# A new instruction order for four engines of a cosine-similarity attention kernel

## The chip, the cores and the metric

The kernel runs on one core of a Trainium2 chip. The metric is the device time of one execution in microseconds (us), as a median over repeated runs. The kernel before takes 190.19 us (median of 3 runs, 190.16 to 190.32).

## What is computed

Q, K and V have 8 batches of 12 heads, each 512 x 64 in float32.

```python
Q_norm = Q / (np.linalg.norm(Q, axis=-1, keepdims=True) + 1e-10)
K_norm = K / (np.linalg.norm(K, axis=-1, keepdims=True) + 1e-10)
scores = np.einsum('bhqd,bhkd->bhqk', Q_norm, K_norm) / tau        # tau = 0.1
weights = np.exp(scores - np.max(scores, axis=-1, keepdims=True))
weights = weights / (np.sum(weights, axis=-1, keepdims=True) + 1e-10)
return np.einsum('bhqk,bhkd->bhqd', weights, V)
```

Scores of normalised rows lie between -10 and 10, so the kernel leaves out the maximum.

## The kernel before

The 96 heads are worked off as 48 pairs of heads, numbered 0 to 47. Each pair goes through the same chain of small operations, and each operation has a key, which this document writes as a name with numbers: `EXP 5.2` is the exponential of pair 5, key block 2.

| name | engine | what it does | line |
|---|---|---|---|
| LD s.0, LD s.1, LV s | SP queue | loads Q, K (256 KB each) and V of pair s | L315, L318 |
| SQ s.0 | POOL (GpSimd) | squares of Q and K | L341 |
| SSQ s.1 | PE (TensorE) | eight matmuls that add up the squares of K, in part | L358 |
| RED s.0, RED s.1 | DVE (VectorE) | row sums of the squares: of Q over the whole (L369), of K over what SSQ left (L365) | L369, L365 |
| NEW g.0 to g.8 | DVE | inverse square root for a group g of 1, 2 or 4 pairs, in small steps, nearly each of which reads what the one before it wrote | L394 to L403 |
| SCL s.0, SCL s.1 | DVE, POOL | Q and K of pair s times their inverse norms; Q on DVE, K on POOL (in nine pairs on DVE) | L427 |
| TR s.0, TR s.1 | PE | four transposes each | L433 |
| EVA s | DVE | copies the transposed pair from PSUM to SBUF | L441 |
| SCO s.c | PE | two matmuls: scores of key block c, for both heads | L532 |
| EXP s.c | ACT (ScalarE) | exponential of that block, 128x1024 | L548 |
| VC s | POOL | V to bf16 | L553 |
| PV s.h.i | PE | four matmuls: weights times V for head h, query block i | L565 |
| RCP s.h, NRM s.h | DVE | one over the sum of the weights; the output times it | L576, L578 |
| ST s | SP queue | stores the pair (256 KB) | L582 |

Some dependences matter below. SCO needs a free one of two double banks of scores, so `SCO n` waits until the exponential two places before it has ended. `SCO s.0` needs EVA s, which needs TR s.0 and TR s.1, which need SCL s.0 and SCL s.1, and these need NEW, RED and SQ. A PV chain has one bank for each head: `PV s.h.0` needs NRM s-1.h. `NRM s` writes into one of eight output buffers and needs the store ST s-8 to have landed. An SQ writes into one of six buffers, and a load LD s into one of 17, so LD s waits for SCL s-17.

Each engine works through a list of operations in a fixed order, and an operation that waits holds up all that stand behind it on that engine or queue. The lists stand in the program as numbers, in the constant `ORDER`, one text for each of sp, pool, dve, pe and act. `schedule` turns the numbers into operations, and `run` works out the semaphores from the operations' needs. Costs and due times that the operations carry are no longer used for the order. Before the first pair stands a head (pair 0 and the first operations of pairs 1 to 3), with warm-up matmuls and fillers on PE.

Of the kernel before, what the change touches and what calls it, by code (L numbers as in the profile page):

```python
# [669 lines left out]
def slack(s, most):  # L670
# [13 lines left out]
    ),  # L684
    "pool": (
# [7 lines left out]
    ),  # L693
    "dve": (
# [23 lines left out]
    ),  # L718
# [78 lines left out]
```

## Time and profile before

| | |
|---|---|
| median of 3 runs | 190.19 us |
| span of the profiled execution | 189.9 us |
| first and last start of EXP on 128x1024 (186 of them) | 12.9 and 184.5 us |
| loads and stores | 50.76 MB, 267 GB/s over the span |

A page of the profile gives the busy time of each engine, the span cut in 40 slices with the busy tenths of each and the granted clock of PE ("PEclk"), the chain of work that ended last, and groups of instructions. A row of a group reads: line, engine, operation, output <- inputs, shapes, xcount | busy us, mean ns of one | idle time of the engine just before them and what ended it. A row of a timeline reads: start in us, duration in us, engine, line, operation, tiles, shapes, xcount, and in brackets an idle time of the engine before it with what ended it. Neighbours of one kind are merged into one row. A row of the windows gives a stretch, its length, and then the busy us and number of instructions of PE, PEld (weight loads), DVE, ACT and POOL, and last the granted clock, the share of the DMA engines and GB/s. A row of a line's own view gives the number of its instructions, their shortest, median and longest duration in ns, and the first and last start.

### The profile page before, as it was taken

To read this page: it belongs to the slowest core of one execution; us is meant where nothing else is said; L and a number is where in the kernel's file an instruction comes from. 1 tells how busy PE (TensorE), PEld (TensorE's weight loads), DVE (VectorE), ACT (ScalarE), POOL (GpSimd) and SP (SyncE) were. 2 spreads that over 40 slices of the span, in tenths; PEclk is the share of its full clock that TensorE was granted. 3 is DMA by queue.
4 is the path that set the end of the run, shared out by engine and by line. 5 is a ranking of instruction groups with operands and counts; after the bars stand their busy time and mean duration, and the time that the engine had idled before them with its cause. 6 is when DMAs were issued, how large, how long until landed. Compare 5 with 4: busy or idle time off the path is not lost.

```text
span 189.9 us, 6666 instructions
## 1 busy us (share of the span) xinstructions
PE 175.6 (92%) x2714; PEld 109.3 (58%) x2714; DVE 170.1 (90%) x552; ACT 183.0 (96%) x215; POOL 161.7 (85%) x150
## 2 busy tenths in 40 slices
PE   7989699999999999999899999899999899897973
PEld 2555356656655666666566566566656565464642
DVE  2699979999999999999997998999999999988642
ACT  5799989999999999999999999999999999999994
POOL 5599987999999999999999999999999994893000
PEclk9999879999999999999999999999999999999999
DMA  5999999999994789999979999999950414000555
GB/s 157 340 358 348 347 349 373 364 369 293 324 384 166 209 270 344 358 369 374 370 238 284 325 383 368 358 366 364 383 200 5 166 59 166 3 0 3 198 194 166
DMA packets 52446, 50.76 MB, mean 267 GB/s; under 512 B 3136, under 2 KB 52416, under 8 KB 52416
## 3 DMA queue, kind: packets, MB, share of 16 engines
q1 hardware_dynamic: 51984, 50.02, 79.7%
q8 instruction: 21, 0.34, 0.7%
q10 hardware_dynamic: 432, 0.33, 0.5%
q14 instruction: 9, 0.07, 0.1%
HBM read 37.75 MB, written 12.58 MB: 265 GB/s over the span
## 4 chain that ended last, share of the span: by engine, by line
ACT 34%; POOL 28%; DVE 20%; PE 8%; DMA 3%; issue 3%; SPq 3%; POOLq 0%
ACT et L548 31%; POOL sq L341 16%; POOL qn L427 6%; POOL vb L553 5%; DVE qn L427 4%; DVE ob L578 3%; DMA out_dram<-ob 3%; DVE qt L441 3%; DVE nps L369 3%; PE scps L532 2%; PE ops L191 2%; ACT et L524 2%; PE ops L565 2%; SPq L315 1%; DVE rd L576 1%
## 5 line engine op out<-in xcount | busy, mean ns | idle before, releaser
L548 ACT ACTIVATE et<-scps 128x1024 bf16<-128x1024 f32 x186 | 171.8, 1104 | 0.8 <-PE scps L532 0.7
L341 POOL TENSOR_TENSOR sq<-qk 128x1024 bf16<-128x1024 f32 x44 | 83.2, 1900 | 0.1
L532 PE MATMUL scps<-qt 64*128 64x512 bf16 x374 | 73.6, 389 | 6.1 <-ACT et L548 3.4
L565 PE MATMUL ops<-vb,et 128*128 128x65 bf16 x1504 | 73.2, 195 | 1.8 <-DVE ob L578 1.2
L565 PEld LDWEIGHTS ops<-vb,et 128*128 128x128 bf16 x1504 | 55.7, 98 | 31.2 <-issue 18.1
L427 POOL TENSOR_TENSOR qn<-qk,rk 128x512 bf16<-128x512 f32 x38 | 39.5, 1048 | 5.8 <-PE scps L532 3.7
L578 DVE TENSOR_TENSOR ob<-ops,rd 128x256 f32<-128x256 f32 x94 | 38.6, 416 | 0.8
L427 DVE TENSOR_TENSOR qn<-qk,nps 128x512 bf16<-128x512 f32 x56 | 37.1, 675 | 0.7 <-ACT nps L386 0.6
L433 PE MATMUL tps<-ident,qn 128*128 128x128 bf16 x376 | 33.9, 221 | 1.1 <-POOL qn L427 0.5
L441 DVE COPY qt<-tps 128x1024 bf16<-128x1024 bf16 x47 | 32.0, 680 | 0.4 <-PE tps L433 0.4
L369 DVE TENSOR_REDUCE nps<-sq 128x8 f32<-128x512 bf16 x46 | 30.8, 681 | 1.0 <-POOL sq L341 0.8
L532 PEld LDWEIGHTS scps<-qt 64*128 64x128 bf16 x374 | 18.2, 93 | 23.4 <-ACT et L548 9.0
L553 POOL TENSOR_SCALAR vb<-vf 128x512 bf16<-128x512 f32 x48 | 29.8, 633 | 0.2 <-PE scps L532 0.2
L433 PEld LDWEIGHTS tps<-ident,qn 128*128 128x128 bf16 x376 | 21.7, 98 | 12.6 <-issue 6.0
L576 DVE RECIPROCAL rd<-ops 128x4 f32<-128x4 f32 x94 | 15.9, 173 | 6.9 <-PE ops L565 5.9
L358 PE MATMUL ops<-sq,ident 128*128 128x64 bf16 x384 | 19.0, 194 | 0.1
L358 PEld LDWEIGHTS ops<-sq,ident 128*128 128x128 bf16 x384 | 14.5, 98 | 2.7 <-issue 1.8
L365 DVE TENSOR_REDUCE nps<-ops 128x8 f32<-128x64 f32 x46 | 10.0, 217 | 0.6 <-PE ops L358 0.5
L394 DVE TENSOR_TENSOR nps<-nps,ys 128x32 f32<-128x32 f32 (+2 forms) x34 | 7.0, 207 | 0.4
L395 DVE SCALAR_TENSOR_TENSOR nps<-nps,ys 128x32 f32<-128x32 f32 (+2 forms) x34 | 7.0, 206 | 0.4
L335 POOL TENSOR_TENSOR sq<-qk 128x512 bf16<-128x512 f32 (+1 forms) x5 | 4.7, 955 | 2.2 <-DMA qk<-in_K_dram 1.9
L191 PE MATMUL ops<-warm_in,ident 128*128 128x512 bf16 x8 | 3.6, 631 | 1.4 <-POOL eps L184 1.4
(66 smaller groups left out, 61.2 us busy)
## 6 DMA issues: line engine op xcount, KB each, us to landing
vf<-in_V_dram SPq DMA_DIRECT2D x48, 256.0 KB, 6.5
qk<-in_Q_dram SPq DMA_DIRECT2D x47, 256.0 KB, 5.5
qk<-in_K_dram SPq DMA_DIRECT2D x47, 256.0 KB, 6.5
out_dram<-ob SPq DMA_DIRECT2D x47, 256.0 KB, 5.8
qk<-in_Q_dram SPq DMA_DIRECT2D x2, 128.0 KB, 2.6
qk<-in_K_dram ACTq DMA_DIRECT2D x2, 128.0 KB, 2.8
out_dram<-ob SPq DMA_DIRECT2D x1, 128.0 KB, 1.7
out_dram<-ob SPq DMA_DIRECT2D x1, 64.0 KB, 1.6
```

The costliest lines, as they stand in the source:

```text
L341: lambda e: e.tensor_tensor(out=sqf, in0=data, in1=data, op=ALU.mult))
L358: last = e.matmul(out=o_ps[bank][:, 320:384], lhsT=ident[:, :], rhs=sq[iqs][:, 8 * w : 8 * w + 8, 8 * k : 8 * k + 8], start=(k == 0), stop ...
L369: lambda e, w=w, dst=dst: e.tensor_reduce(out=dst, in_=sq[iqs][:, 8 * w : 8 * w + 8, :], axis=AX.X, op=ALU.add))
L427: lambda e, w=w, r=r: e.tensor_tensor(out=qn[iqn][:, w].rearrange("p t h d -> p h t d"), in0=qk[iq][:, w].rearrange("p h (t d) -> p h t d" ...
L433: last = e.transpose(t_ps[:, w, t, :], qn[iqn][:, w, t].rearrange("p h d -> p (h d)"), ident[:, :])
L441: lambda e: e.tensor_copy(out=qt[iqt][:, :, :, :].rearrange("p w t x -> p (w t x)"), in_=t_ps[:, :, :, :].rearrange("p w t x -> p (w t x)")))
L532: last = e.matmul(out=sc_ps[:, 2 * b + h, :], lhsT=qt[iqt][64 * h : 64 * h + 64, 1, c, :], rhs=qt[iqt][64 * h : 64 * h + 64, 0, :, :], sta ...
L548: lambda e, c=c, b=b: e.activation(out=et[iet][:, c, :, :], in_=sc_ps[:, 2 * b : 2 * b + 2, :], func=ACT.Exp, scale=math.log(2.0) / UNIT i ...
L553: lambda e: e.tensor_scalar(out=vb[:, iq, :, :, 0:DIM].rearrange("p c h d -> p h c d"), in0=vf[iv][:, :, :].rearrange("p h (c d) -> p h c ...
L565: last = e.matmul(out=o_ps[h][:, 65 * t : 65 * t + 65], lhsT=et[iet][:, c, h, 128 * t : 128 * t + 128], rhs=vb[:, iq, c, h, :], start=(c = ...
L576: lambda e, h=h, grid=grid: e.reciprocal(out=rd[io][:, h, :], in_=grid[:, :, DIM]))
L578: lambda e, h=h, grid=grid: e.tensor_tensor(out=ob[io][:, h], in0=grid[:, :, 0:DIM], in1=rd[io][:, h, :].unsqueeze(2).to_broadcast([128, N ...
```

## The change

The change replaces four of the five texts in `ORDER`: those of SP, POOL, DVE and PE. The text of ACT holds the same numbers in the same order. No operation is added or taken out, and none changes its engine, its shape or its needs. The first entries (21 on SP, 17 on POOL, 26 on DVE, 34 on PE) are the same; behind them nearly every entry stands at another place. The orders are said to come from a new search that used measured spacings of operations and put a price on stretches in which PE is seldom busy.

Cut to its first lines, with the numbers of the operations:

```diff
     "sp": (
-        "7 8 70 71 109 110 11 154 155 72 198 199 111 241 242 156 275 276 200 317 318 243 351 352 277 394 395 319 428 "
+        "7 8 70 71 109 110 11 154 155 72 198 199 111 241 242 156 275 276 200 317 318 395 243 429 319 394 352 351 504 277 "
...
     "pool": (
-        "0 1 2 4 17 31 26 75 112 113 157 158 56 95 201 244 173 184 140 278 250 320 227 261 303 354 292 326 397 380 "
+        "0 1 2 4 17 31 26 75 112 113 157 158 56 95 201 244 173 278 140 184 227 320 250 397 354 292 326 261 303 337 431 "
...
     "dve": (
...
-        "129 164 165 166 131 167 202 168 204 169 170 171 245 247 205 206 61 207 175 208 209 210 67 212 211 213 214 "
-        "216 68 62 218 248 106 281 107 279 321 252 323 282 151 283 152 284 100 285 101 286 287 289 288 290 145 355 "
+        "164 165 166 167 131 168 202 169 204 170 171 245 247 67 205 68 206 207 175 208 61 209 62 210 211 212 281 213 214 "
+        "216 248 106 218 107 100 279 101 321 323 151 282 152 283 284 252 285 286 145 287 146 288 289 290 355 189 324 294 "
...
     "pe": (
...
-        "182 102 103 104 105 280 219 251 221 249 147 148 223 149 150 322 96 225 97 98 99 253 191 192 193 194 255 141 "
+        "97 98 180 215 217 182 99 219 147 148 149 221 150 322 251 223 249 141 225 142 191 143 144 253 192 255 185 186 "
```

Read as names, the stretches that the prediction speaks of are these. On PE, from SCO 2.3 to SCO 4.0:

```diff
-SCO2.3 SCO3.0 SCO3.1 SCO3.2 TR4.0 TR4.1 SCO3.3 PV1.1.0 PV1.1.1 PV1.1.2 PV1.1.3 SSQ6.1 SCO4.0
+SCO2.3 PV1.1.0 PV1.1.1 PV1.1.2 PV1.1.3 SCO3.0 SSQ6.1 SCO3.1 PV1.0.0 PV1.0.1 PV1.0.2 SCO3.2 TR4.0 TR4.1 SCO3.3 PV1.0.3 SCO4.0
```

On DVE, from RED 5.1 to EVA 4:

```diff
-RED5.1 NEW4.0 NEW4.1 RCP0.0 NEW4.2 EVA3 NEW4.3 NEW4.4 NEW4.5 RCP0.1 NEW4.7 NEW4.6 NEW4.8 SCL4.0 SCL4.1 NRM0.1 NRM0.0 EVA4
+RED5.1 RCP0.1 NEW4.0 NRM0.1 NEW4.1 NEW4.2 EVA3 NEW4.3 RCP0.0 NEW4.4 NRM0.0 NEW4.5 NEW4.6 NEW4.7 RED6.1 NEW4.8 SCL4.0 SCL4.1 SCL5.0 RCP1.1 EVA4
```

On POOL, from SCL 3.1 to SQ 10.0:

```diff
-SCL3.1 VC3 VC2 SQ6.0 SCL5.1 SQ7.0 VC4 VC5 VC6 SQ8.0 SCL6.1 SCL7.1 SQ9.0 VC8 VC9 SQ10.0
+SCL3.1 SQ6.0 VC2 VC3 VC4 SQ7.0 SCL5.1 SQ9.0 SQ8.0 SCL6.1 SCL7.1 VC5 VC6 VC7 SQ10.0
```

On the SP queue the loads and stores no longer stand in the order of the pairs. ST 12, for example, moves from the 108th place to the 94th and ST 13 from the 100th to the 118th. In the new order LD 34.1, LD 35.1, LD 37.0 and LD 37.1 stand at the 96th, 100th, 105th and 108th place, ahead of ST 13 (122nd, 125th, 132nd and 134th before), and ST 10, 76th before, is the 92nd.

143 rows, old and new, of the table ORDER are left out of this document.

## The prediction

> **What bounds the kernel now.** I read the page first, for the busy shares and the clock, then the view of L548, the exponential, then stretches of the head by windows, and last the timelines of PE, DVE and POOL there.
>
> ```profile
> span 189.9 us, 6666 instructions
> ...
> PE 175.6 (92%) x2714; PEld 109.3 (58%) x2714; DVE 170.1 (90%) x552; ACT 183.0 (96%) x215; POOL 161.7 (85%) x150
> ...
> PEclk9999879999999999999999999999999999999999
> ...
> L369 DVE TENSOR_REDUCE nps<-sq 128x8 f32<-128x512 bf16 x46 | 30.8, 681 | 1.0 <-POOL sq L341 0.8
> ...
> vf<-in_V_dram SPq DMA_DIRECT2D x48, 256.0 KB, 6.5
> ```
> ```profile
> L548 ACT ACTIVATE et<-scps x186: 1017/1095/1263, 12.9 to 184.5; 128x1024 bf16<-128x1024 f32 x186
> ...
> L548 ACT ACTIVATE et<-scps x22: 1018/1149/1263, 40.9 to 59.9; 128x1024 bf16<-128x1024 f32 x22
> ...
> L548 ACT ACTIVATE et<-scps x29: 1017/1055/1166, 12.9 to 39.9; 128x1024 bf16<-128x1024 f32 x29
> ```
>
> ACT is busy 96% of the span, and its list doesn't change. What can change is the waiting between its exponentials. The second row of L548 shows the pace when nothing is late: 21 steps in 59.9 - 40.9 = 19.0 us, 0.905 us each (one overlaps the next, so the duration of 1.1 us is not the pace). At that pace the 185 steps of the first row take 167.4 us, and they took 171.6. So 4.2 us of waiting is all that an order can win behind the first EXP; the time can't fall below about 186. The third row says where it lies: 28 steps (25.3 us) took 27.0 up to EXP 8.0, the first of pair 8, which is 1.7 us of waiting in the head; the other 2.5 us is spread over 157 steps.
>
> The windows of the head show what happens there:
>
> ```profile
> 19.06:22.47 3.41, 1.88 (x16) 0.83 (x16) 3.34 (x14) 3.41 (x5) 3.41 (x4) 1.00 1.10 348
> 22.47:25.88 3.41, 3.41 (x36) 2.05 (x35) 2.92 (x8) 2.66 (x4) 3.41 (x5) 0.50 1.10 347
> 25.88:29.30 3.42, 3.42 (x68) 2.42 (x66) 2.71 (x13) 3.41 (x4) 1.80 (x1) 1.00 1.10 349
> 179.49:182.90 3.41, 2.43 (x42) 1.39 (x40) 1.73 (x6) 3.41 (x5) 0.00 (x0) 1.00 1.03 342
> ```
>
> For 3.41 us from 22.47 PE's granted clock is 0.50, right behind a stretch in which PE was busy 1.88 of 3.41 us (55%). A stretch with 2.43 (71%) late in the kernel was followed by no such drop: the row PEclk of the page falls below 9 in its fifth and sixth slice alone. ACT, always busy else, is busy 2.66 of 3.41 us while the clock is halved.
>
> **The change part by part: the head.** The timeline of PE shows the thin stretch, and that of DVE what hung on it:
>
> ```profile
> 19.72 0.39 PE L532 MATMUL scps<-qt 64*128 64x512 bf16 x2 [0.71 <-DVE qt L441]
> ...
> 21.37 0.39 PE L532 MATMUL scps<-qt 64*128 64x512 bf16 x2 [0.53 <-ACT et L548]
> 21.69 0.62 PE L433 MATMUL tps<-ident,qn 128*128 128x128 bf16 x8
> ...
> 28.50 0.67 PE L565 MATMUL ops<-vb,et 128*128 128x65 bf16 x16
> 29.10 0.39 PE L532 MATMUL scps<-qt 64*128 64x512 bf16 x2
> 29.42 0.66 PE L565 MATMUL ops<-vb,et 128*128 128x65 bf16 x16
> ...
> 30.34 0.41 PE L358 MATMUL ops<-sq,ident 128*128 128x64 bf16 x8
> 30.58 0.61 PE L433 MATMUL tps<-ident,qn 128*128 128x128 bf16 x8
> 31.12 0.39 PE L532 MATMUL scps<-qt 64*128 64x512 bf16 x2
> ```
> ```profile
> 18.16 0.22 DVE L365 TENSOR_REDUCE nps<-ops 128x8 f32<-128x64 f32 x1
> 18.42 0.19 DVE L403 TENSOR_SCALAR ys<-nps 128x32 int32<-128x32 int32 x1
> 18.64 0.20 DVE L394 TENSOR_TENSOR nps<-nps,ys 128x32 f32<-128x32 f32 x1
> ...
> 18.99 0.68 DVE L441 COPY qt<-tps 128x1024 bf16<-128x1024 bf16 x1
> 19.58 0.18 DVE L399 SCALAR_TENSOR_TENSOR ys<-nps,ys 128x32 f32<-128x32 f32 x1
> ...
> 21.77 0.75 DVE L578 TENSOR_TENSOR ob<-ops,rd 128x256 f32<-128x256 f32 x2
> ...
> 24.20 0.18 DVE L576 RECIPROCAL rd<-ops 128x4 f32<-128x4 f32 x1 [0.49 <-PE ops L358]
> ...
> 26.21 0.69 DVE L441 COPY qt<-tps 128x1024 bf16<-128x1024 bf16 x1 [0.18 <-PE tps L433]
> 27.37 0.23 DVE L365 TENSOR_REDUCE nps<-ops 128x8 f32<-128x64 f32 x1 [0.47 <-PE ops L358]
> ...
> 38.78 0.68 DVE L441 COPY qt<-tps 128x1024 bf16<-128x1024 bf16 x1
> ```
>
> From the score pair at 19.72 to the transposes at 21.69 PE has nothing but score pairs to do. The new PE list puts the PV groups of pair 1 there: PV 1.1.0 to 1.1.3 ahead of SCO 3.0, SSQ 6.1 behind it, PV 1.0.0 to 1.0.2 behind SCO 3.1. From the full-speed rows four PV groups take 0.60 us (28.50 to 29.10), an SSQ 0.24 (30.34 to 30.58). The seven PV groups and the SSQ are 1.05 + 0.24 = 1.3 us, so PE's busy time in that stretch goes from 1.88 to about 3.0 us at most; I take 2.6, since SCL 4.1 and with it TR 4.1 come later (below). That is 76%, above the 71% that kept the clock.
>
> Their data must be there. PV 1.1.0 needs NRM 0.1, which ran at 21.77 because the order put it behind SCL 4.1. In the new DVE list RCP 0.1 follows RED 5.1 (18.16), and NRM 0.1 ends about 18.97. SSQ 6.1 needs SQ 6.0, which POOL began at 19.32, behind two VC; the new POOL list has SQ 6.0 ahead of them:
>
> ```profile
> 18.15 1.21 POOL L553 TENSOR_SCALAR vb<-vf 128x512 bf16<-128x512 f32 x2
> 19.32 1.90 POOL L341 TENSOR_TENSOR sq<-qk 128x1024 bf16<-128x1024 f32 x1
> ...
> 25.78 1.90 POOL L341 TENSOR_TENSOR sq<-qk 128x1024 bf16<-128x1024 f32 x1
> 29.67 2.04 POOL L427 TENSOR_TENSOR qn<-qk,rk 128x512 bf16<-128x512 f32 x2 [1.99 <-DVE rk L399]
> ```
>
> So SQ 6.0 starts near 18.15 and ends near 20.0, in time. POOL's one hole, 1.99 us before SCL 6.1, is closed as well: SQ 9.0 stands ahead of SQ 8.0 and three VC go behind. I cost that at nothing, as POOL isn't what pair 8 waits for.
>
> What pair 8 waits for is DVE. EVA 8 starts at 38.78 and EXP 8.0 at 39.9, 1.2 us later: copy, score pair, exponential with nothing between. One row holds DVE's work from RED 5.1 up to there:
>
> ```profile
> 18.16:38.78 20.62, 18.91 (x282) 11.83 (x280) 19.11 (x71) 19.86 (x22) 18.63 (x19) 0.92 1.10 358
> ```
>
> DVE is busy 19.11 of 20.62 us, idle 1.51. Three terms follow.
>
> First, the waits for PE of 0.49, 0.18 and 0.47 us at 24.20, 26.21 and 27.37, all of work that was begun at half clock. An operation that waits for nothing starts 0.09 us before the end of the one ahead (18.99 + 0.68 - 19.58), so each wait costs 0.09 more: 1.14 + 0.27 = 1.41 us. It goes if the clock stays up.
>
> Second, an operation that reads its predecessor's result starts 0.03 us after the end (18.42 + 0.19 to 18.64), 0.12 later than an independent one. Counted in the two lists up to EVA 8, 11 neighbours of that kind become 8: 0.36 us less.
>
> Third, one operation more stands ahead of EVA 8, RED 10.0: 0.68 - 0.09 = 0.59 us. Small new waits I take at 0.1 us: SCO 3.0 comes 0.25 us later, for NRM 0.1 now stands ahead of EVA 3, and EVA 4 comes later too, for the two NRM and RED 6.1 stand ahead of SCL 4.0 and SCL 4.1; but DVE itself loses nothing by that.
>
> The sum is -1.41 - 0.36 + 0.59 + 0.1 = -1.1 us at EXP 8.0. It can't be better than -1.5, all of DVE's idle time; if the clock halves as before it is +0.3.
>
> **The rest.** Behind EXP 8.0, 2.5 us of waiting is spread thin. A score pair holds PE for 0.32 us (29.10 to 29.42), so the pace of 0.905 us leaves 0.585 us between two of them. Four PV groups take 0.60, a TR four 0.27 (half of 30.58 to 31.12). I counted the two lists with these prices, for the 157 gaps from EXP 8.0 on: more than 0.60 us of work stands in 39 gaps before and in 30 after, more than 0.80 us in 5 before and in none after. A late score pair costs nothing while ACT still has an exponential to run, so a gap alone doesn't stall; it does where the data is late too. If the waiting goes with the number of full gaps, 2.5 x 30 / 39 = 1.9 us stays: -0.6 us. The ends: nothing of it gained, or down to 1.0 us (-1.5), as no order so tight has none. It can also grow, which is a rival.
>
> The tail holds the same operations in nearly the same order, so nothing there. The sum is 189.9 - 1.1 - 0.6 = 188.2 us of span. The median was 0.3 us above the span (190.19 to 189.9), so the forecast is 188.5 us.
>
> **A rule beside the clock.** The rows say that 55% busy in one 3.41 us stretch is too little and 71% is enough. The Trainium skill, page "TensorE: Matmul & The Clock Gate", section "Part 1: The HAM clock gate", has a window of 3413 ns, which the 3.41 us of the trace fits, but names an idle window as what throttles; here the stretch was 55% busy, so the trace decides. It also says that the windows run freely and don't start with the kernel. That speaks against relying on one place, and is the second rival.
>
> **The rivals.** *Given back behind the head.* In the new list the second TR of a pair stands only one gap ahead of its SCO s.0 for ten pairs from pair 9 on (seven before). Such a pair must run TR, EVA and SCO within two paces, 1.81 us, and 0.27 + 0.68 + 0.39 leaves under half a microsecond for DVE to be free; an SCL or RED in front (0.59) takes that. At 0.17 us for each of the ten it is +1.7, and all is as before: 190.2 us. For it speaks that DVE is busy nearly all the time, against it that SCL and NEW also stand earlier.
>
> *The clock halves anyway*, because the window that counts lies otherwise, for instance across 17.5 to 20.9 and 20.9 to 24.3, or because NRM 0.1 or NRM 0.0 come later than I worked out. Then the first term is gone: +0.3 - 0.6 gives 189.9 us.
>
> *The stores hold up DVE*, which would end slower. NRM 21 needs ST 13 landed. The chain before has such a wait already, NRM 20 for ST 12:
>
> ```profile
> 85.28 6.47 DMA out_dram<-ob
> 91.77 0.42 DVE ob L578
> ...
> 92.03 1.07 SPq L318 DMA_DIRECT2D vf<-in_V_dram  x2
> ...
> 95.58 0.41 DVE L578 TENSOR_TENSOR ob<-ops,rd 128x256 f32<-128x256 f32 x1
> ```
>
> ST 12 moves up, ST 13 falls back to the 118th place, behind loads that wait for SCL 17.1, 18.1 and 20.1. The 118th issue before (the second of those at 92.03, about 92.5) would put its landing 6.5 us later, at 99. NRM 21 began at 95.58 and would now want to begin near 94.5. It would stand 4.5 us, and everything behind it on DVE with it; ACT would feel some 2.5 of that once its stock of scores is used up, so 188.5 + 2.5 = 191.0 us. The point is a landing of ST 13 later than 94.5. Against it: the queue isn't held at ST 10 at the 76th place any more, so it should reach the 118th several us sooner.
>
> *Better than forecast*: the waiting behind the head falls to 1.0 us, 187.6 us.
>
> **How the numbers follow.** Chances: forecast 0.53; better 0.14; given back 0.10; clock halves anyway 0.10; stores or another queue, slower 0.13. A measurement of this kernel can tell about 0.2% (0.4 us) from no change. The forecast and the better case are faster (0.67), of the clock case half (0.05), and of the given-back case a third (0.04): 0.76 faster. The rest of these two, 0.11, is the same or a little slower: 0.10 same, and 0.14 slower with the stores. The range reaches from 187.1 (-1.5 and -1.5 with rounding) to 190.3, just above the case in which all is given back, and leaves out the stores.
>
> **What would show it.** Right: no 0.5 in the clock behind 20 us, PE busy near 2.6 of 3.41 us in 19.06 to 22.47; EXP 8.0 near 38.8; DVE without the three waits; POOL without its hole at 28 to 30. Then the starts of the L548 row should span about 169.9 us in place of 171.6. Wrong: a stretch at half clock anywhere; NRM rows released by the store's DMA; score pairs that wait for EVA behind pair 9 by more than before.

## The result, and the profile after

The kernel after takes 193.52 us (median of 4 runs, 192.16 to 193.91), beside 190.25 us for the kernel before (4 runs, 190.16 to 191.66). The ratio is 1.0144, 95% interval 1.0096 to 1.0193 (that of the two medians alone would be 1.017). It was forecast faster, at 188.5 us, with a range up to 190.3. It is slower, outside the range.

From the page of the kernel after, the busy shares, the granted clock, and the traffic in 40 slices of 4.8 us:

```profile
span 190.3 us, 6690 instructions
...
PE 175.2 (92%) x2714; PEld 109.2 (57%) x2714; DVE 172.2 (90%) x552; ACT 182.3 (96%) x215; POOL 163.0 (86%) x150
...
PEclk9999999999999999999999999999999999999998
...
GB/s 161 345 350 352 349 368 353 379 353 302 210 351 353 341 379 299 347 357 326 347 383 374 379 165 262 303 269 181 233 370 232 0 3 0 3 103 285 166 69 267
```

The view of the exponential's line, over the whole and up to EXP 8.0:

```profile
L548 ACT ACTIVATE et<-scps x186: 1017/1140/1277, 12.9 to 183.8; 128x1024 bf16<-128x1024 f32 x186
...
L548 ACT ACTIVATE et<-scps x29: 1017/1056/1098, 12.9 to 38.7; 128x1024 bf16<-128x1024 f32 x29
```

The windows of the head, at the same places as before:

```profile
19.06:22.47 3.41, 2.95 (x48) 1.80 (x49) 3.35 (x14) 3.41 (x5) 3.41 (x5) 1.00 1.10 348
22.47:25.88 3.41, 3.06 (x45) 1.73 (x46) 3.41 (x12) 3.41 (x4) 3.41 (x3) 1.00 1.10 355
```

Up to here nearly everything is as forecast. PE is busy 2.95 us where it was 1.88, the clock stays at 1.00, and EXP 8.0 starts at 38.7 (39.9 before, 38.8 forecast). Even the last exponential on 128x1024 starts earlier, at 183.8 in place of 184.5. And yet the span is 0.4 us longer, although this is the fastest of the four executions (192.16): what was won had been lost again by the end, and some of it behind the last of these exponentials.

To find the places I took, in each trace, the starts of the 186 exponentials, and counted as waiting what an interval between two of them is above the pace of 0.904 us. The last column is the time from the last of them to the end of the span, which the page and the row of L548 give as well (190.3 - 183.8):

| kernel | first EXP | to pair 8 | pairs 8 to 12 | 13, 14 | 15 to 39 | 40 on | last start | to the end |
|---|---|---|---|---|---|---|---|---|
| before | 12.95 | 1.69 | 0.02 | 0.20 | 1.85 | 0.55 | 184.50 | 5.37 |
| after | 12.95 | 0.47 | 0.13 | 1.13 | 1.28 | 0.59 | 183.79 | 6.55 |

Two columns got clearly worse: pairs 13 and 14, by 0.9 us, and the stretch behind the last exponential, by 1.2 us. Together they undo the 1.2 us of the head and the 0.6 of the middle, with some left over.

**Pair 13.** In the timeline of ACT in the kernel after, the exponential at 58.65 is EXP 13.1:

```profile
58.65 1.02 ACT L548 ACTIVATE et<-scps 128x1024 bf16<-128x1024 f32 x1 [0.49 <-PE scps L532]
```

Its score pair (L532) stands on PE behind an SSQ (L358), and that waits for POOL:

```profile
57.88 0.41 PE L358 MATMUL ops<-sq,ident 128*128 128x64 bf16 x8 [0.78 <-POOL sq L341]
58.22 0.39 PE L532 MATMUL scps<-qt 64*128 64x512 bf16 x2
```

On POOL the square (L341) that this needs ran behind a V cast that began late. (The two upper rows show that POOL's old hole at 28 to 30 is closed, as forecast.)

```profile
24.64 3.75 POOL L341 TENSOR_TENSOR sq<-qk 128x1024 bf16<-128x1024 f32 x2
28.34 2.04 POOL L427 TENSOR_TENSOR qn<-qk,rk 128x512 bf16<-128x512 f32 x2
...
51.86 1.89 POOL L341 TENSOR_TENSOR sq<-qk 128x1024 bf16<-128x1024 f32 x1
55.34 0.63 POOL L553 TENSOR_SCALAR vb<-vf 128x512 bf16<-128x512 f32 x1 [1.58 <-PE ops L565]
55.93 1.89 POOL L341 TENSOR_TENSOR sq<-qk 128x1024 bf16<-128x1024 f32 x1
```

POOL stood still for 1.58 us before VC 15 (55.34). The timeline names PE as the releaser, but the view of POOL's waits puts most of it down to a load:

```profile
POOL vb L553 <- DMA vf<-in_V_dram: 1.3, 1, 1.3
```

LV 15 landed at 55.26. Why so late stands in the timeline of the SP queue, a row of which runs from the issue of its first transfer to that of its last; the stretch between two rows is the queue waiting:

```profile
41.92 1.79 SPq L315 DMA_DIRECT2D qk<-in_K_dram  x2
47.48 1.72 SPq L318 DMA_DIRECT2D vf<-in_V_dram  x2
...
140.63 28.11 SPq L582 DMA_DIRECT2D out_dram<-ob  x3
168.77 0.47 SPq L318 DMA_DIRECT2D vf<-in_V_dram  x1
...
172.17 14.30 SPq L582 DMA_DIRECT2D out_dram<-ob  x9
186.52 1.44 SPq L616 DMA_DIRECT2D out_dram<-ob  x2
```

From 43.7 to 47.48 nothing is issued. The next entry, at the 61st place, is LV 19, whose buffer comes free with VC 10. Two lists made this wait: the new POOL list puts VC 10 back (from the 33rd place to the 43rd), where it ended at 47.46, and the new SP list moves LV 19 forward (from the 71st place) and LV 15 back (from the 55th to the 64th), behind it. So the queue stood for 3.8 us ahead of LV 15.

**The end.** The same view shows three stores in one row of 28.11 us. The last of the three is ST 39, whose turn on the queue comes at 142.37 and which waits for NRM 39.1 until 168.36. Behind it stand stores of earlier pairs (38, 34, 35, 37 and 36), and further down three more (44, 43 and 40) behind ST 45, which waits for NRM 45.1 until 183.74. In the page's row of GB/s, slices 32 to 35 hold 0, 3, 0, 3. The stores then go out in one heap. The kernel before has long waits for stores' data too. Here is that row of the queue's own waits (total, number, longest), before and after:

```profile
SPq L582 <- DVE ob L578: 30.4, 8, 15.8
```
```profile
SPq L582 <- DVE ob L578: 34.4, 7, 26.0
```

The 15.8 us of the kernel before are at ST 42, with four stores of earlier pairs behind it (39, 40, 38 and 41). But that wait ended at 174.9, early enough for the heap to go out under the last exponentials. In the kernel after the wait at ST 45 ended at 183.74, with 44, 43 and 40 still behind it. Here is the traffic from 180 to 190 us in 40 slices of a quarter of a us, first of the kernel before, then after:

```profile
GB/s 336 360 336 320 377 311 320 418 311 369 311 250 33 33 49 29 25 20 0 0 0 0 0 0 0 127 336 340 352 340 360 250 320 205 264 242 10 0 0 0
...
DMA packets 2047, 1.84 MB, mean 184 GB/s; under 512 B 146, under 2 KB 2045, under 8 KB 2045
```
```profile
GB/s 0 0 0 0 0 0 0 0 66 33 0 0 0 0 0 0 0 0 90 336 344 352 315 373 332 307 377 332 324 377 332 320 360 348 340 318 263 154 0 0
...
DMA packets 1794, 1.60 MB, mean 160 GB/s; under 512 B 128, under 2 KB 1792, under 8 KB 1792
```

Before, over half of the bytes are out by 183, and the rest goes from 186.25 to 189. After, 1.6 MB go out from 184.5 to 189.5 at some 340 GB/s, and the kernel waits for them. The last operation on ACT ended 0.77 us earlier than before (its last store is issued at 186.99, 187.76 before), and the kernel ended 0.4 us later.

The kernel before has executions of two kinds. The profile holds the span and the mean granted clock of each execution, and 36 of 99 executions of the kernel before that the groups of runs below list have a clock of 0.988 to 0.991, the others 0.995 to 1.0. A stretch of 3.41 us at half clock costs 3.41 / 2 / 190 = 0.009 of the mean, so the former are those with the halved stretch of the head. They take 1.0 to 1.5 us longer: medians 192.05 to 190.53, 191.83 to 190.47 and 191.51 to 190.53 in the three groups. The profile of before that the prediction read is one of these.

### The profile page after: what moved, and what is told of

The parts are those of the page before. It is cut to its first block, busy times and chain, and to the rows that moved or that the text cites. A ratio compares the mean times of both kernels' runs of the same rounds, so it can differ in the third digit from the quotient of the medians.

```text
span 190.3 us, 6690 instructions
## 1 busy us (share of the span) xinstructions
PE 175.2 (92%) x2714; PEld 109.2 (57%) x2714; DVE 172.2 (90%) x552; ACT 182.3 (96%) x215; POOL 163.0 (86%) x150
## 4 chain that ended last, share of the span: by engine, by line
ACT 57%; DVE 25%; PE 9%; DMA 4%; POOL 1%; SPq 1%; issue 1%; DVEq 0%; POOLq 0%
ACT et L548 56%; DVE qn L427 5%; DVE ob L578 4%; DVE qt L441 4%; DVE nps L369 3%; PE ops L565 3%; PE scps L532 3%; DMA qk<-in_Q_dram 2%; DMA out_dram<-ob 1%; PE tps L433 1%; DVE nps L394 1%; DVE nps L395 1%; DVE rd L576 1%; DVE et L490 1%; DVE nps L365 1%; POOL sq L341 1%
## 5 line engine op out<-in xcount | busy, mean ns | idle before, releaser
L548 ACT ACTIVATE et<-scps 128x1024 bf16<-128x1024 f32 x186 | 171.2, 1137 | 0.7 <-PE scps L532 0.7
L341 POOL TENSOR_TENSOR sq<-qk 128x1024 bf16<-128x1024 f32 x44 | 82.9, 1894 | 0.2 <-DMA qk<-in_K_dram 0.2
L532 PE MATMUL scps<-qt 64*128 64x512 bf16 x374 | 72.9, 386 | 6.1 <-ACT et L548 2.5
L565 PE MATMUL ops<-vb,et 128*128 128x65 bf16 x1504 | 74.7, 194 | 1.3 <-DVE ob L578 0.7
L565 PEld LDWEIGHTS ops<-vb,et 128*128 128x128 bf16 x1504 | 56.3, 98 | 30.9 <-issue 18.8
L433 PE MATMUL tps<-ident,qn 128*128 128x128 bf16 x376 | 34.8, 221 | 0.6 <-POOL qn L427 0.2
L553 POOL TENSOR_SCALAR vb<-vf 128x512 bf16<-128x512 f32 x48 | 30.7, 653 | 3.0 <-PE ops L565 1.6
L532 PEld LDWEIGHTS scps<-qt 64*128 64x128 bf16 x374 | 18.4, 92 | 22.9 <-ACT et L548 8.4
L358 PE MATMUL ops<-sq,ident 128*128 128x64 bf16 x384 | 19.0, 193 | 0.9 <-POOL sq L341 0.8
L358 PEld LDWEIGHTS ops<-sq,ident 128*128 128x128 bf16 x384 | 14.3, 98 | 3.5 <-issue 2.3
```

The lines of the kernel that those rows point to most:

```text
L341: lambda e: e.tensor_tensor(out=sqf, in0=data, in1=data, op=ALU.mult))
L358: last = e.matmul(out=o_ps[bank][:, 320:384], lhsT=ident[:, :], rhs=sq[iqs][:, 8 * w : 8 * w + 8, 8 * k : 8 * k + 8], start=(k == 0), stop ...
L433: last = e.transpose(t_ps[:, w, t, :], qn[iqn][:, w, t].rearrange("p h d -> p (h d)"), ident[:, :])
L532: last = e.matmul(out=sc_ps[:, 2 * b + h, :], lhsT=qt[iqt][64 * h : 64 * h + 64, 1, c, :], rhs=qt[iqt][64 * h : 64 * h + 64, 0, :, :], sta ...
L548: lambda e, c=c, b=b: e.activation(out=et[iet][:, c, :, :], in_=sc_ps[:, 2 * b : 2 * b + 2, :], func=ACT.Exp, scale=math.log(2.0) / UNIT i ...
L553: lambda e: e.tensor_scalar(out=vb[:, iq, :, :, 0:DIM].rearrange("p c h d -> p h c d"), in0=vf[iv][:, :, :].rearrange("p h (c d) -> p h c ...
```

## The experiments

Two theories stood against each other: that the SP queue's new order alone spoils what the other lists gain, or that the other lists lose it on PE and DVE. The runs were made in three groups, and times are compared within a group. The kernel before took 190.75 us in the first (e1 to e4, 23 runs, 190.10 to 192.56), 191.25 in the second (e5 to e8, 35 runs, 189.97 to 192.77) and 190.68 in the third (e9 to e12, 29 runs, 190.17 to 192.41).

**e1, the changed kernel once more.** No edit.

> The changed kernel once more, on one chip with the kernel before. The profiled spans differ by 0.4 us only (190.3 to 189.9) while the medians differ by 3.3, so either the chips or sessions differ, or the changed kernel varies from run to run. If the sessions differ: ratio near 1.003 (190.3 / 189.9). If the loss is real in every run: ratio near 1.015.

192.42 us (191.75 to 194.16, 6 runs), ratio 1.0105 [1.0055, 1.0155]. Its trace has the two places again: 1.16 us of waiting in pairs 13 and 14, and 6.59 us behind the last start. So neither was a chance of the one profile.

**e2, the SP list of before under the new PE, DVE and POOL lists.**

```diff
     "sp": (
-        "7 8 70 71 109 110 11 154 155 72 198 199 111 241 242 156 275 276 200 317 318 395 243 429 319 394 352 351 504 277 "
+        "7 8 70 71 109 110 11 154 155 72 198 199 111 241 242 156 275 276 200 317 318 243 351 352 277 394 395 319 428 "
...
```

> The new orders of PE, DVE and POOL with the SP queue's order of before. Theory A, the SP queue's order loses the time (a hold at LV 19 near 45 us, and stores that pile up behind the last exponential): the gain of the head stays and the two losses go, so about 1.7 us under the kernel before, ratio 0.991. Theory B, the new orders of the three engines lose it themselves: no better than the changed kernel, ratio above 1.0.

202.03 us (200.97 to 204.71, 6 runs), ratio 1.0586 [1.0535, 1.0638]. From its view of waits:

```profile
ACT et L548 <- PE scps L532: 8.9, 9, 4.4
...
POOL sq L341 <- DMA qk<-in_K_dram: 5.9, 5, 4.5
...
DVE ob L578 <- DMA out_dram<-ob: 4.7, 3, 2.4
```

ACT waits 8.9 us. The longest stretch is ahead of EXP 26.0, 4.65 us above the pace, where POOL waits 4.51 us for a load of pair 34; the square of pair 31 stands behind that on POOL, and its SSQ stands on PE ahead of SCO 26.0. The new lists of the engines ask for loads at other times than the old SP list brings them, so the theory that the SP list is the one bad part of four falls in this form: SP had to change with them. What stays possible is that it was changed badly at a few places, and those the next runs mend one at a time.

**e3, the last 20 entries of SP in turn.**

```diff
-LV47 ST33 ST32 ST39 LV43 ST38 ST34 ST35 LV45 ST41 ST42 ST37 ST36 ST45 ST44 ST43 ST40 ST46 ST47.0 ST47.2
+LV47 LV43 LV45 ST32 ST33 ST34 ST35 ST36 ST37 ST38 ST39 ST40 ST41 ST42 ST43 ST44 ST45 ST46 ST47.0 ST47.2
```

> The changed kernel, with only the last 20 entries of the SP queue put in turn: LV 47, LV 43 and LV 45 first, then ST 32 to ST 47 in the order of the pairs, so that no store waits behind ST 39 or ST 45. Theory A: the last store lands about 1 us earlier and NRM 44 no longer waits for a store; 1.2 us less than the changed kernel. Theory B: within 0.3 us of it.

191.11 us (190.31 to 192.82, 12 runs), ratio 1.0007 [0.9975, 1.0039]; 1.3 us less than e1. In its profile the last start is at 183.23 and the span 188.6, so 5.38 us are left at the end, as in the kernel before. The tail's price is shown.

**e4, LV 19 and LV 22 later,** behind entries that don't wait.

```diff
-LD23.1 LV19 LV22 LD19.1 LV15
+LD23.1 LD19.1 LV15
...
-LD23.0 LD26.1
+LD23.0 LV19 LV22 LD26.1
```

> The changed kernel, with only LV 19 and LV 22 moved on the SP queue from ahead of LD 19.1 and LV 15 to behind LD 23.0, so that the queue isn't held for VC 10 at 43 to 47.5 us. Theory A: LV 15 lands near 51 in place of 55.3, VC 15 and SQ 16.0 don't wait, the exponentials of pair 13 keep their pace; 1.1 us less than the changed kernel. Theory B: SSQ 16.1 is late anyway as POOL is behind; within 0.3 us of it.

192.03 us (191.21 to 194.13, 12 runs), ratio 1.0060 [1.0033, 1.0087]; only 0.4 us less than e1, which is within the intervals of the two. In the timeline of POOL the hole ahead of VC 15 is gone (the cast at 54.01, which ran at 55.34):

```profile
52.15 1.89 POOL L341 TENSOR_TENSOR sq<-qk 128x1024 bf16<-128x1024 f32 x1
54.01 0.62 POOL L553 TENSOR_SCALAR vb<-vf 128x512 bf16<-128x512 f32 x1
54.60 1.89 POOL L341 TENSOR_TENSOR sq<-qk 128x1024 bf16<-128x1024 f32 x1
```

and the waiting of pairs 13 and 14 falls from 1.16 to 0.04 us. That this hold made that stall is shown. But the time didn't follow by as much: in this trace 0.4 us of waiting stands at EXP 23.3, which e1 doesn't have, and 0.5 us more in the head.

**e5, both edits.**

> The changed kernel with both edits to the SP queue of the two runs before: the last stores in turn, LV 19 and LV 22 later. Theory A (the loss is the queue's order, in two places): both gains add, about 1.7 us less than the changed kernel, so 190.7 us, level with the kernel before. Theory B (the three other orders lose it): not under 191.5.

191.13 us (190.01 to 191.73, 12 runs), ratio 0.9998 [0.9970, 1.0027], no more than e3 had alone. Its waits show who took the place of the first stall:

```profile
DVE ob L578 <- DMA out_dram<-ob: 2.1, 2, 1.3
```
```profile
96.32 0.42 DVE L578 TENSOR_TENSOR ob<-ops,rd 128x256 f32<-128x256 f32 x1 [0.84 <-DMA out_dram<-ob]
```

NRM 21 (96.32) waits for ST 13, and NRM 33 for ST 25; EXP 23.3 and EXP 35.3 come 0.8 and 0.9 us late for it (in this trace, which is of e5's slowest execution, 191.73). This is the rival of the stores in the prediction. In the changed kernel ACT had been held up ahead of them already, and they cost little.

**e6, the kernel before once more,** and **e7, the kernel before with the head's filling alone:** the PE and DVE stretches of the change shown above (from SCO 2.3 and from RED 5.1), and on POOL only

```diff
-SCL3.1 VC3 VC2 SQ6.0 SCL5.1
+SCL3.1 SQ6.0 VC3 VC2 SCL5.1
```

> The kernel before, with a profile of its own. Its executions fall in two kinds by the granted clock: about 0.989 at spans of 189.7 to 190.6, and 0.995 to 1.0 at 188.1 to 189.1; the profile that the prediction was made from was of the first kind. If the half-clock stretch near 22 us is what sets them apart, a profile of the second kind shows no 0.5 there and EXP 8.0 at 38.5 to 39.0 in place of 39.9. If it is something else, EXP 8.0 stays at 39.9 and the time is won elsewhere.

> The kernel before with the head's part of the change alone: PV groups of pair 1 put between SCO 2.3 and SCO 3.3 on PE, NRM 0.1 and NRM 0.0 earlier on DVE, SQ 6.0 ahead of two VC on POOL; SP and all the rest as before. Theory A: the spans of 189.7 to 190.6 go, the others stay as they are, so the median falls by 0.1 to 0.5 us and the highest by 1.5. Rival: the filling delays EVA 3 and EVA 4 in every run by 0.2 to 0.5 us, and the median rises by that.

e6: 190.86 us (190.39 to 191.83, 12 runs), ratio 1.0000 [0.9976, 1.0025], with a clock of 0.991 or less in 4 of 12. Its profile is one of the four, and the windows around its halved stretch are these:

```profile
18.02:21.43 3.41, 1.98 (x17) 0.65 (x15) 3.27 (x15) 3.41 (x5) 3.41 (x5) 1.00 1.10 348
21.43:24.84 3.41, 3.41 (x38) 2.29 (x36) 2.50 (x8) 2.45 (x3) 3.41 (x4) 0.50 1.10 347
```

The halved stretch begins at 21.43 here and at 22.47 in the first profile, each time behind 3.41 us in which PE is busy under 2 us.

e7: 190.70 us (190.29 to 191.84, 12 runs), ratio 0.9989 [0.9959, 1.0019]. No execution of the 12 has a clock under 0.995. The same two places in its windows:

```profile
19.06:22.47 3.41, 3.04 (x48) 1.77 (x46) 3.34 (x15) 3.41 (x5) 3.41 (x4) 1.00 1.10 348
18.02:21.43 3.41, 3.18 (x50) 1.88 (x49) 3.34 (x18) 3.41 (x5) 3.37 (x4) 1.00 1.11 349
```

The filling does keep the clock up. But 190.70 is no better than the 190.47 of those executions of before, in the same group, whose clock wasn't halved. The filling takes the bad kind of execution away and wins nothing over the good kind.

**e8, seven entries more moved on SP:** e5, with LD 23.0, ST 3, ST 13 and ST 25 further forward, to where they are ready, and LV 25, LV 41 and LV 42 further back, behind loads that don't wait. Each is shown at its new place, below the entry ahead of it.

```diff
 LD23.1
+LD23.0
...
 LV14
+ST3
...
 LD24.1
+LV19 LV22
...
 LV23
+LV25
...
 LD35.1
+ST13
...
 ST22
+LV41
...
 ST24
+ST25
...
 LD46.0
+LV42
```

> The kernel of both edits, with six more entries of the SP queue moved, each of which held the queue or came late in the profile after: LD 23.0 up behind LD 23.1, ST 3, ST 13 and ST 25 up to where they are ready, LV 25, LV 41 and LV 42 down behind loads that don't wait. Theory A: no exponential waits for a load or store any more; another 0.5 to 1.0 us less than with both edits, 189.9 us, under the kernel before by 0.8. Theory B: no different from both edits.

190.02 us (189.84 to 190.92, 12 runs), ratio 0.9937 [0.9910, 0.9965]: faster than both kernels. It is 1.1 us less than e5, and 0.7 less than e7. The page, the line of the exponential, the SP queue's end and the traffic from 180 to 190 us:

```profile
span 188.1 us, 6690 instructions
...
PEclk9999999999999999999999999999999999999998
```
```profile
L548 ACT ACTIVATE et<-scps x186: 1017/1219/1297, 13.0 to 182.7; 128x1024 bf16<-128x1024 f32 x186
```
```profile
139.46 45.45 SPq L582 DMA_DIRECT2D out_dram<-ob  x15
185.36 0.83 SPq L616 DMA_DIRECT2D out_dram<-ob  x2
```
```profile
GB/s 0 0 0 0 29 373 336 283 29 33 0 0 8 8 180 356 356 180 25 0 0 66 332 356 307 336 201 281 217 2 0 0 0 0 0 0 0 0 0 33
```

The starts span 182.7 - 13.0 = 169.7 us, where the prediction wanted 169.9, and the span is 188.1, where it wanted 188.2. The stores go out one by one as they are ready, and the last bytes are written at 187.3 (189.5 in the kernel after). Its DVE never waits for a store. It isn't free of holds on the queue: the row of waits that was shown above reads 34.2 us here, as much as in the kernel after, but in 13 waits, the longest of 6.1. So it isn't the waiting of the queue as such that costs; what costs is an entry behind it that could have gone and that something needs soon.

**e9, e8 with the last 20 entries of SP as in the change, e10, e8 with the thin PE and DVE stretch of before** (SSQ 6.1 and PV 1.x back behind SCO 3.3, DVE as before from RED 5.1 to EVA 4 and SCL 5.0, RCP 1.1, RED 6.1 behind it), **e11, e8 again, and e12, the changed kernel again.**

> The same kernel, with only the last 20 entries of the SP queue put back as the changed kernel has them (behind ST 39, ST 41, ST 42 and ST 45). If the pile of stores at the end costs what the profile after shows, 6.55 us from the last whole exponential to the end in place of 5.37: 1.2 us more, 191.2 us. If it was only a follow-up of the other waits, within 0.3 us of the base.

> The same kernel with the head's thin stretch put back on PE and DVE as in the kernel before (SCO 3.0 to SCO 3.2 without PV groups between them). If the filling is what keeps the clock up: a third to a half of the executions show a clock of about 0.99 and spans 1 to 1.5 us longer, the others stay at the base. If the clock depended on something else: no such executions, and the median within 0.3 us of the base.

> The kernel with all the held or late entries of the SP queue moved, once more, as the base for the two kernels that follow on this chip: again about 190.0 us, ratio to the kernel before 0.994.

> The changed kernel itself on this chip, for its spread: medians of 193.5 and 192.4 us so far, with spans from 190.0 to 192.2. If the loads and stores that arrive just in time are what spreads it: again 192 to 194, while the base, with the same orders of PE, DVE and POOL, stays within 1.1 us.

| kernel | us (lowest to highest, runs) | ratio to before | waiting to pair 8, 8 to 12, 13 and 14, 15 to 39, 40 on | to the end |
|---|---|---|---|---|
| e11 | 190.03 (189.39 to 191.13, 12) | 0.9950 [0.9925, 0.9975] | 1.37, 0.13, 0.04, 1.27, 0.56 | 5.38 |
| e9 | 191.54 (191.07 to 192.42, 12) | 1.0045 [1.0024, 1.0065] | 0.69, 0.13, 0.04, 1.27, 0.81 | 6.55 |
| e12 | 192.75 (192.23 to 194.02, 6) | 1.0114 [1.0076, 1.0153] | 0.63, 0.13, 0.77, 1.18, 0.81 | 6.58 |
| e10 | 191.12 (190.46 to 192.12, 12) | 1.0025 [1.0001, 1.0048] | 1.04, 0.13, 0.03, 1.27, 0.56 | 5.38 |

e9 is 1.5 us above e11, with the end back at 6.55 us and NRM 44 again behind a store. e12 is 1.2 us above e9: they differ in the nine entries moved ahead of the tail alone. So the path from the better kernel back to the changed one is split and measured, 190.03 + 1.5 + 1.2 = 192.75. (The profile of e11 is its slowest execution, 191.13 us, so its 1.37 isn't typical of it; e8 has 0.47.) The runs of e11 spread over 1.7 us and those of e12 over 1.8, so that the late loads and stores aren't what spreads the changed kernel.

e10 has a clock of 0.989 or 0.990 in 3 of 12, as it should with the thin stretch back. But its other nine have a median of 190.86, 0.8 above e11, so that here the old order of that stretch costs something even where the clock isn't halved; I hadn't expected that. The profile is one of those nine:

```profile
19.06:22.47 3.41, 1.84 (x16) 0.64 (x13) 3.27 (x16) 3.41 (x5) 3.41 (x5) 1.00 1.10 348
17.44:20.86 3.42, 2.68 (x32) 1.34 (x30) 3.29 (x14) 3.42 (x5) 3.42 (x3) 1.00 1.09 350
20.86:24.27 3.41, 2.55 (x42) 1.53 (x40) 3.40 (x11) 3.41 (x5) 3.41 (x5) 1.00 1.10 349
```

1.84 us of 3.41 at one place are followed by a full clock here. The traces tell why. In each of the 14, the records of the clock begin with a first one at full clock, and every later change lies a whole number of 3.41 us behind its start. That start is 5.41 in the first profile and 4.37 in e6, and the halved stretch begins five such windows later (22.47 and 21.43). In e10 it is 7.20, so the windows are those of the second and third row: the boundary at 20.86 parts the thin stretch, and neither half is low enough.

## Why the prediction was wrong, by its own steps

**What bounds the kernel, and the pace: right.** ACT's pace stayed 0.904 us, and all the kernels differ in waiting and in the end.

**The baseline: failed.** The prediction put it so: "The median was 0.3 us above the span (190.19 to 189.9)". In every execution of which both are known, the time is 1.7 to 2.1 us above the span (192.16 to 190.3 in the changed kernel's profiled one). A span of 189.9 belongs to a time of about 191.7, and the fourth run of the kernel before, which wasn't among the three that the forecast had, took 191.66. So the profile that the whole sum was made on wasn't of an execution like the median one: it had the halved stretch, and the three runs of 190.16 to 190.32 didn't. A sum of 188.2 us of span is a time of 190.0, not 188.5. That is what e8 and e11 have, 190.02 and 190.03.

**The head: the mechanism right, its worth not.** PE busy 2.95 us where 2.6 was forecast, a full clock, EXP 8.0 at 38.73 against 38.8, DVE's waits and POOL's hole gone: every sign that the prediction named for the head came out. Clocks of 0.992 or less are found in 3 of 100 executions of the ten kernels with the filled stretch (the changed one, e1, e3 to e5, e7 to e9, e11 and e12; e2, whose long stalls halve the clock elsewhere, is left out), against 36 of 99 of before. But the -1.41 us for the three waits is won only where there was a halved stretch, so in about a third of the executions and not in the median one. Without that term the prediction's own working leaves +0.3 for the head (-0.36 + 0.59 + 0.1), and e7 against the unhalved executions of before is 190.70 - 190.47 = +0.2.

**The rest, -0.6 us by counting gaps: right in size, but not for the reason given.** From pair 8 on, 2.62 us of waiting before became 2.00 in e8 (0.13 + 0.03 + 1.27 + 0.57). e8 is 0.7 us below e7, which has the same filling in the head. In the changed kernel the stretch from pair 15 to 39 already shows it, 1.28 to 1.85. But the waiting didn't go with the number of full gaps. Priced as the prediction has it, the exponentials right behind a full gap wait 1.14 us in the first profile, where there are 39 of them, and 1.10 in e8, where there are 30; it is at the others that 1.48 became 0.91. That the size came out is luck in so far, and which part of the new lists won it was not tried. The rival *given back*, by transposes only one gap ahead, didn't happen.

**"The tail holds the same operations in nearly the same order, so nothing there": failed.** The last stores are out of turn in both lists, but in the new one ST 44, 43 and 40 stand behind ST 45, whose data are ready only at 183.74. In the old one a single store, ST 45, stands behind so late an entry (ST 46, 185.5), and the heap behind ST 42 was let go at 174.9. It costs 1.2 us in the profiles (6.55 to 5.37) and 1.3 to 1.5 in the medians (e3 to e1, e9 to e11).

**POOL's hole "costed at nothing", and the queues: failed.** What SQ 9.0 and the others moved up push back is the casts, VC 10 among them, and LV 19 waits for VC 10 at the 61st place of the queue. I had followed ST 13 and the loads ahead of it through the queue, and not the other entries that wait. The queue's waits for casts (L553), before and after, show it:

```profile
SPq L318 <- POOL vb L553: 2.4, 3, 1.6
```
```profile
SPq L318 <- POOL vb L553: 20.4, 9, 5.5
```

The longest are at LV 41 (5.5 us), LV 42 (5.1), LV 19 (3.8) and LV 25 (3.3). The nine entries that were moved ahead of the tail, these four among them, cost 1.2 us together (e9 to e12). With LV 19 and LV 22 moved already, the other seven still cost 1.1 us (e5 to e8), and in e5's trace ACT waits for the two late stores among them, ST 13 and ST 25.

**The rival of the stores: right in its mechanism, wrong in its price.** ST 13 landed at 96.04, past the 94.5 that was to decide, and NRM 21 followed at 96.13. But where it was to cost 2.5 us, DVE's four waits for stores come to 1.6 us in the whole trace:

```profile
DVE ob L578 <- DMA out_dram<-ob: 1.6, 4, 0.7
```

ACT lost nearly nothing by them: from pair 15 to 39 it waits 1.28 us there, and 1.27 in e8, in which no operation of DVE waits for a store. Only with that hold gone (e5) were they felt, as 0.8 and 0.9 us. The reason given against the rival, that the queue would no longer be held at ST 10, was no reason: it was held elsewhere.

So the sum that the runs bear out is 190.2 to 190.5 us (before, not halved) + 0.3 for the head - 0.6 for the rest, which is the 190.0 of e8, + 1.3 to 1.5 for the tail + 1.2 for the holds: 192.5 to 192.7, beside 192.42 in e1 and 192.75 in e12. The 193.52 of the first four runs lies above that and within the range of e1; what the other 0.8 us are is not known.

**What stays open.** How much each of the seven moves of e8 is worth was not tried one by one. Why e4 gained 0.4 us where its trace lost 1.1 of waiting is explained by the new waits only in the one execution that was profiled. The profiles differ by up to 1.3 us in the start of the first EXP (12.5 in e4 to 13.8 in e10), though all lists begin alike, and the waiting of the head differs between e8 and e11, which are one kernel (0.47 and 1.37); no run tells what makes these differences. And why the thin stretch costs 0.8 us without a halved clock in e10, where the filling won nothing over the unhalved executions of before in e7, isn't settled: no profile of such an execution of before was had.

## What to carry to other kernels

Before one profile becomes the ground of a sum, set its span beside its own time and look at the clock of the other executions: a stretch that only some executions have isn't a gain in the median. When an order is searched anew, go through every in-order queue entry by entry, write down what each entry waits for and when that now ends, and see who stands behind it and how soon it is needed; one load that waits for a buffer holds up loads that need nothing. And look behind the last exponential too: stores that are ready go out only when the store ahead of them is. A long wait costs nothing when it ends early enough, as at ST 42 before; what still stands behind the last wait is added to the end.

## What the runs showed of the hardware

*Whether a thin stretch halves the clock depends on where the windows of 3.41 us lie in that execution.* In all 14 traces, the windows counted from the first record at full clock that were followed by half clock had PE busy 1.98 us (58%, in e6) or less, and those that kept the full clock had 2.10 us (61%, in e2) or more; no trace has one between. This row of e9 is near the limit, and the clock stayed full behind it to the end:

```profile
183.18:186.60 3.42, 2.12 (x49) 1.63 (x46) 1.90 (x8) 2.34 (x6) 0.00 (x0) 1.00 0.84 276
```

In the first profile and in e10, windows with 1.98 us or less would have to begin within a stretch of 1.33 us, of 3.41 possible, which is 39%; that is an estimate from two traces, and the runs have 36 of 99 and 3 of 12. The Trainium skill, page "TensorE: Matmul & The Clock Gate", section "Part 1: The HAM clock gate", says that the window of 3413 ns runs freely and doesn't start with the kernel. The runs agree: the first full clock begins anywhere from 4.1 to 7.2 us in the 14 traces. The section names an idle window as what throttles; here more than half of the window was busy.

*What stands behind a waiting entry goes out in one heap.* While ST 39 stood on the SP queue for 26.0 us the DMA engines moved 0 to 3 GB/s in four slices of 4.8 us, with finished outputs waiting behind it; at the end 1.6 MB took 5 us at some 340 GB/s, the last 2.5 of them with nothing computed any more (ACT ends at 187.0).
